# Operand sums of an MLP's first products taken in two column parts, and a token tile's transposes moved in among matmuls

## The chip, the core and the metric

The kernel runs on one NeuronCore of a Trainium2 chip. The engines are TensorE (PE, with its weight loads shown as PEld), VectorE (DVE), ScalarE (ACT) and GpSimd (POOL); SyncE (SP) issues the DMAs. Each engine works through its own queue in order and waits on semaphores for the others. The metric is device time in microseconds of one execution, median of several runs; lower is better.

## What is computed

One encoder layer over 1024 tokens of width 1024, all float32. The part that matters here is the end of the mixing stage and the start of the MLP:

```
x = x + (gate_a * y_a + gate_b * y_b) @ w_out
h = rmsnorm(x, norm_mlp_g)
x = x + square(relu(h @ w_ff1)) @ w_ff2        # w_ff1: 1024 x 4096
```

After the MLP a gated per-layer embedding is added and the result is normalised.

## The kernel before, in words

Every float32 product is made from three matmuls of a reduced-precision pair: `split` (lines 234 to 236) writes a rounded high part on ACT and the remainder, the low part, on DVE, and `mm3` (lines 241 to 248) does high x high, high x low and low x high.

**End of the mixing stage** (`mix_outputs`, from line 973). The gated sum `m` (1024 channels, transposed) is multiplied by `w_out` for eight token tiles of 128 tokens. A tile takes 48 matmuls (eight k-steps of six). Then DVE adds the residual (line 1050), SP stores it (`s_x`), and `scale` (line 1026) normalises the rows: a square with row sums on ACT (line 264), a chain of twelve 128x1 operations on DVE (lines 265 and 253 to 258), and a scaled copy on DVE (line 1028) into a tile of `fx`. `turn(t)` (line 1030) transposes that scaled tile with eight matmuls into PSUM (line 1034), and two copies on ACT (line 1036) spread it over four buffers `hf`, which hold h transposed: f11 and f21 are the first and second half of the channels for tokens 0 to 511 (tiles 0 to 3), f12 and f22 the same for tokens 512 to 1023 (tiles 4 to 7). `turn(t - 1)` is written behind the matmuls of tile t, and `turn(7)` behind everything.

Low and high parts of `w_out` rows 4 to 7 stand in slots 0 to 3 of the six-slot ring `wc`; slots 4 and 5 are unused in this stage.

**Start of the MLP** (`up`, from line 1062). h @ w_ff1 is done by a Winograd scheme of seven half-size products for each job of 256 columns (16 jobs). On the weight side `early` (line 144) loads a job's weights, takes four sums s1 to s4 on POOL (lines 151 to 154) and splits the job's own left half, s1 and s2; `late` (line 160) splits s3, s4 and one more quarter. Splits go to `wc`, which `up` takes in the order of slots 0 to 5. On the side of h the operands are the splits of f11 and f21 (b11, b21; buffers `ha`), of f22 and of f12 - f11 (b22, t1; `hb`), and of three further sums (t2, t3, t4; `hc`). The sums are taken in place, over all 512 columns of a buffer at once:

```
f11 = f12 - f11   (DVE, line 1096)      f22 = f22 - f11   (DVE, line 1101)
f12 = f22 - f12   (POOL, line 1099)     f21 = f22 - f21   (DVE, line 1104)
```

Products 1 and 2 need b11 and b21, product 5 t1, product 6 t2, 7 t3, 3 b22, 4 t4. The first two jobs, a and b, are interleaved: products 1 and 2 of a, of b, then 5 of both, then 6 of both (lines 1106 to 1109), then the rest of a and of b. `ha`, `hb` and `hc` lie over the buffers `m`, `rwt` (the split `m` tiles) and `wo` plus `fx` of the mixing stage, and come free when those do.

**What orders the work.** The kernel is written in program order; a planner assigns each engine's queue before the run. [...] Once planned, a queue is fixed: an instruction that waits holds back everything behind it on its engine. A block `tc.manual_schedule(engines={PE})` keeps PE's instructions of that block in the order in which they are written.

Of the kernel before, what the change touches and what calls it, by code (L numbers as in the profile page):

```python
# [14 lines left out]
ALU = mybir.AluOpType  # L15
# [5 lines left out]
NT = S // P  # L21
KD = D // P
# [203 lines left out]
class Layer:  # L226
# [79 lines left out]
    def run(self):  # L306
        tc, nc, io = self.tc, self.nc, self.io
        base = Region(tc, "base", F32, "left")
        self.ident = base.take(128)
        make_identity(nc, self.ident)  # L310
        self.small = base.ring(8, 16)
        self.bg = base.take(16)
        self.rq = base.take(64)
        self.qss = base.take(64)
        self.qtmp = base.take(64)
        raw = base.take(4096)
        self.raw = Ring([raw[:, 1024 * i:1024 * i + 1024] for i in range(4)])
        self.raw2 = Ring([raw[:, 2048 * i:2048 * i + 2048] for i in range(2)])
        self.gain = base.ring(1, 1024)
        self.g_ring = Ring([base.take(1024), self.gain.slots[0]])  # L320
        pad = Region(tc, "pad", F32, "right")
        pad.take(8)
        psum = Region(tc, "psum", F32, None, space=bass.MemoryType.PSUM)
        self.psum = psum.take(4096)
        self.bank = [self.psum[:, i * 512:(i + 1) * 512] for i in range(8)]
        self.bank2 = [self.psum[:, i * 1024:(i + 1) * 1024] for i in range(4)]

        self.mix_inputs()
        self.attend_a()
        self.mix_outputs()  # L330
        self.wg, self.rg = [], []
        self.up()
        self.down()
        self.ple()
        pad.close()
        psum.close()
        base.close()
# [635 lines left out]
    def mix_outputs(self):  # L973
        tc, nc, io = self.tc, self.nc, self.io
        rm, rwt, wo0 = (Region(tc, n, d, "left") for n, d in (("m", F32), ("rwt", F32R), ("wo", F32R)))
        self.left = [rm, rwt, wo0]
        m = v3(rm.take(8192), KD)
        wt = rwt.ring(8, 1024)
        wo = [(wo0.take(1024), wo0.take(1024)) for _ in range(4)]
        fg = Region(tc, "fg", F32, "right")  # L980
        g_ring = fg.ring(4, 1024)
        ps_r = Ring(self.bank2)
        for c in range(KD):
            wa = self.w_chunk(io["w_out_a"][0], c * P, wt)
            raw = v3(self.raw.next()[:, :256], 2)
            self.load(raw, io["w_out_b"][0][:, c * P:(c + 1) * P].rearrange("(k p) c -> p k c", p=P))
            wb = wt.next()
            wb = [v3(wb[:, 256 * i:256 * i + 256], 2) for i in range(2)]
            self.split(wb[0], wb[1], raw)
            ga, gb = g_ring.next(), g_ring.next()  # L990
            self.load(ga, self.dr["gd"][c])
            self.load(gb, self.dr["gd"][KD + c])
            nc.scalar.activation(ga, ga, AF.Sigmoid)
            nc.scalar.activation(gb, gb, AF.Sigmoid)
            ya, yb = ps_r.next(), ps_r.next()
            for k in range(2):
                self.mm3([yb[:, 0:512], yb[:, 512:1024]], (wb[0][:, k, :], wb[1][:, k, :]),
                         [tuple(self.oB[i][:, k, h * 512:(h + 1) * 512] for i in range(2)) for h in range(2)],
                         k == 0, k == 1)
            self.proj_T(ya, wa, self.oA)  # L1000
            nc.vector.tensor_tensor(out=ga, in0=ga, in1=ya, op=ALU.mult)
            nc.vector.tensor_tensor(out=gb, in0=gb, in1=yb, op=ALU.mult)
            nc.vector.tensor_tensor(out=m[:, c, :], in0=ga, in1=gb, op=ALU.add)
        fg.close()
        self.ro.close()

        self.rc = Region(tc, "rc", F32R, "right")
        self.rf = [Region(tc, n, F32, "right") for n in ("rfa", "rfb")]
        fx = Region(tc, "fx", F32, "right")
        self.wc = self.rc.ring(6, 2048)  # L1010
        self.hf = [self.rf[i].take(2048) for i in (0, 1, 1, 0)]
        hf = [v3(a, 4) for a in self.hf]
        self.rs = self.rf[1].take(1024)
        x_ring = fx.ring(4, 1024)
        gm = self.gain.next()
        self.gain_row(gm, io["norm_mlp_g"][0])
        for k in range(KD):
            if k >= 4:
                s = self.wc.next()
                wo.append((s[:, :1024], s[:, 1024:]))  # L1020
            raw = self.raw.next()
            self.load(raw, io["w_out"][0][k * P:(k + 1) * P, :])
            self.split(wo[k][0], wo[k][1], raw)
        ps_m, ps_t = Ring(self.bank2[:2]), Ring(self.bank2[2:])

        def scale(t, x, xs):
            r = self.row_rstd(x, xs)
            nc.vector.scalar_tensor_tensor(xs, x, r, gm, op0=ALU.mult, op1=ALU.mult)

        def turn(t, xs):  # L1030
            sl = slice(t % 4 * P, t % 4 * P + P)
            ps = ps_t.next()
            for k in range(KD):
                nc.tensor.transpose(ps[:, k * P:(k + 1) * P], xs[:, k * P:(k + 1) * P], self.ident)  # L1034
            for i in range(2):
                nc.scalar.activation(hf[2 * i + t // 4][:, :, sl], v3(ps[:, 512 * i:512 * i + 512], 4), AF.Copy)

        for t in range(NT):
            sl = slice(t * P, (t + 1) * P)
            x, xs = x_ring.next(), x_ring.next()  # L1040
            self.load(x, io["x"][0, sl, :])
            mt = [v3(wt.next(), KD) for _ in range(2)]
            for k in ((slice(0, 7), slice(7, 8)) if t < 2 else (slice(0, 8),)):
                self.split(mt[0][:, k, :], mt[1][:, k, :], m[:, k, sl])
            ps = ps_m.next()
            for k in range(KD):
                self.mm3([ps[:, 0:512], ps[:, 512:1024]], (mt[0][:, k, :], mt[1][:, k, :]),
                         [tuple(w[:, h * 512:(h + 1) * 512] for w in wo[k]) for h in range(2)],
                         k == 0, k == KD - 1)
            nc.vector.tensor_tensor(out=x, in0=x, in1=ps, op=ALU.add)  # L1050
            self.load(self.dr["x1"][sl, :], x)
            scale(t, x, xs)
            if t:
                turn(t - 1, last)
            last = xs
        turn(NT - 1, last)
        fx.close()
        for region in self.left[::-1]:
            region.close()


    def up(self):
        tc, nc, io = self.tc, self.nc, self.io
        w1 = io["w_ff1"][0]
        left = []
# [1 line left out]
        def pair_tile(name, n):  # L1067
            region = Region(tc, name, F32R, "left")
            left.append(region)
            return [tuple(v3(region.take(2048), 4) for _ in range(2)) for _ in range(n)]  # L1070

        b11, b21 = pair_tile("ha", 2)
        b22, t1 = pair_tile("hb", 2)
        t2, t3, t4 = pair_tile("hc", 3)
        f11, f12, f21, f22 = (v3(a, 4) for a in self.hf)
        tiles = [a[:, o:o + 1024] for a in (self.hf[i] for i in (0, 3, 1, 2)) for o in (0, 1024)]
        s_hf, s_own = tiles[6:], [self.g_ring.slots[0], self.rs]
# [6 lines left out]
        def job(j):  # L1084
            return j, w1[:, 256 * j:256 * j + 256], relu2, 1

        v = nc.vector
        n_pair = FF // 256
        wi = Winograd(self, Ring([x[:, o:o + 1024] for x in self.wc.slots for o in (0, 1024)]), Ring(self.bank),
                      Ring(tiles[:6]), lambda j: s_hf if j and j % 2 == 0 else s_own,  # L1090
                      {1: b11, 2: b21, 3: b22, 4: t4, 5: t1, 6: t2, 7: t3}, a22_units=2)
        self.split(*b11, f11)
        self.split(*b21, f21)
        x0 = wi.early(*job(0)[:2])
        wi.late(*x0)
        v.tensor_tensor(out=f11, in0=f12, in1=f11, op=ALU.subtract)
        self.split(*t1, f11)
        x1 = wi.early(*job(1)[:2])
        nc.gpsimd.tensor_tensor(out=f12, in0=f22, in1=f12, op=ALU.subtract)
        self.split(*b22, f22)  # L1100
        v.tensor_tensor(out=f22, in0=f22, in1=f11, op=ALU.subtract)
        self.split(*t2, f22)
        self.split(*t3, f12)
        v.tensor_tensor(out=f21, in0=f22, in1=f21, op=ALU.subtract)
        self.split(*t4, f21)
        a, b = wi.pair(0, x0[2], relu2), wi.pair(1, x1[2], relu2)
        for which in (1, 2), (5,), (6,):
            a.mm(*which)
            b.mm(*which)
        a.first()  # L1110
        b.first()
        wi.late(*x1)
# [232 lines left out]
```

## Time and profile before

| | us |
|---|---|
| median of 3 runs | 1818.11 (1815.13 to 1819.92) |
| the profiled execution, its own time | 1816.29 |
| its span in the trace | 1814.5 |
| PE busy in it | 1746.4 (96%) |
| DVE, ACT, POOL busy | 1244.1, 798.4, 425.9 |

PE's busy time counts overlapping matmuls and modelled ends, so a back-to-back stream is read from the starts of its rows, not from their lengths. In a timeline row the two first numbers are start and duration in us; rows merge neighbours of one form (x is how many), and the bracket is the idle time of that engine just before, with what ended it. [...]

### The profile page before, as it was taken

The numbers are of one execution on the slowest core, as the hardware profiler recorded it, in microseconds if no ns is written. First come the engines' busy times: TensorE is split into PE (matmuls) and PEld (weight loads), VectorE is DVE, ScalarE is ACT, GpSimd is POOL, SyncE is SP. The second block draws the span as 40 slices with busy tenths as digits, with TensorE's granted clock in tenths as the row PEclk, the third lists the DMA queues.
The fourth block names the chain that finished last, engine by engine and source line by source line (L and its number), as shares of the span: only waits on it lengthen the run. The fifth ranks groups of instructions, "written<-read, shape, count | busy, mean of one in ns | idle before, by whom it ended". The sixth has DMA issues, their size and how long they took to land.

```text
span 1814.5 us, 22763 instructions
## 1 busy us (share of the span) xinstructions
PE 1746.4 (96%) x8451; PEld 1438.5 (79%) x8451; DVE 1244.1 (69%) x2055; ACT 798.4 (44%) x1383; POOL 425.9 (23%) x236
## 2 busy tenths in 40 slices
PE   6999999998998899999999989999999999989897
PEld 5888888776787788888888778888888888867786
DVE  7556654466764787875445686555569999999564
ACT  6333233366333677775232445353446333332331
POOL 0242332001000000000001134343337676572000
PEclk9999999999999999999999989999999999999899
DMA  6243234565162322215433214332454333331101
GB/s 215 80 162 122 93 128 140 165 217 178 52 182 66 74 41 22 33 19 140 155 128 118 90 61 140 115 114 97 139 207 152 114 106 113 132 128 35 35 36 47
DMA packets 132287, 199.20 MB, mean 110 GB/s; under 512 B 25508, under 2 KB 92932, under 8 KB 132176
## 3 DMA queue, kind: packets, MB, share of 16 engines
q1 hardware_dynamic: 131008, 194.17, 33.5%
q0 software_dynamic: 1168, 3.57, 0.7%
q8 instruction: 67, 1.10, 0.3%
q14 instruction: 44, 0.36, 0.1%
HBM read 146.12 MB, written 54.73 MB: 111 GB/s over the span
## 4 chain that ended last, share of the span: by engine, by line
PE 52%; DVE 13%; issue 2%; ACT 1%; DMA 0%; DVEq 0%; SPq 0%; ACTq 0%
PE psum L239 48%; DVE rc L236 6%; DVE facc L1178 4%; PE psum L910 3%; DVE fsum L1199 1%; DVE rg L236 1%; DVE hb L236 0%; PE psum L275 0%; PE psum L1034 0%; DVE fsum L1224 0%; ACT fp L904 0%; DVE facc L1213 0%; DVE base L900 0%; DVE fy L273 0%; DMA s_qd<-fa 0%
## 5 line engine op out<-in xcount | busy, mean ns | idle before, releaser
L239 PE MATMUL psum<-rc,rc 128*128 128x512 f32 x1464 | 341.9, 394 | 9.2 <-DVE rc L236 8.8
L239 PE MATMUL psum<-rh,rh 128*128 128x512 f32 (+1 forms) x1428 | 337.4, 389 | 1.6 <-ACT rh L235 1.1
L239 PEld LDWEIGHTS psum<-rc,rc 128*128 128x128 f32 x1464 | 278.2, 190 | 69.1 <-DVE rc L236 9.9
L239 PEld LDWEIGHTS psum<-rh,rh 128*128 128x128 f32 x1428 | 261.1, 190 | 59.6 <-issue 5.9
L151 POOL TENSOR_TENSOR base<-base 128x512 f32<-128x512 f32 x17 | 29.7, 1747 | 711.6 <-DMA base<-in_w_ff 534.5
L239 PE MATMUL psum<-ht,rh 128*128 128x512 f32 x624 | 145.7, 389 | 0.0
L239 PE MATMUL psum<-hc,rc 128*128 128x512 f32 x576 | 137.9, 389 | 0.0
L239 PEld LDWEIGHTS psum<-ht,rh 128*128 128x128 f32 x624 | 117.1, 188 | 24.3
L235 ACT ACTIVATE rh<-base 128x512 fp32r<-128x512 f32 (+1 forms) x77 | 61.2, 808 | 148.3 <-PE psum L239 120.5
L239 PEld LDWEIGHTS psum<-hc,rc 128*128 128x128 f32 x576 | 108.1, 188 | 22.5
L236 DVE TENSOR_TENSOR rh<-base,rh 128x512 fp32r<-128x512 f32 (+1 forms) x77 | 77.6, 1017 | 63.8 <-PE psum L239 39.0
L235 ACT ACTIVATE rc<-base 128x1024 fp32r<-128x1024 f32 (+1 forms) x64 | 51.5, 827 | 151.8 <-PE psum L239 147.3
L239 PE MATMUL psum<-ro,rwt 128*128 128x512 f32 x480 | 109.4, 389 | 0.0
L239 PE MATMUL psum<-kv,rq 128*128 128x512 f32 x384 | 101.3, 400 | 6.0 <-ACT rq L235 4.2
L900 DVE TENSOR_REDUCE base<-psum 128x1 f32<-128x1024 f32 x64 | 78.4, 1224 | 39.0 <-PE psum L239 37.5
L239 PEld LDWEIGHTS psum<-ro,rwt 128*128 128x128 f32 x480 | 90.0, 188 | 18.6
L239 PE MATMUL psum<-rp,kv 128*128 128x512 f32 x384 | 104.4, 406 | 0.0
L209 DVE TENSOR_TENSOR fw<-fw,psum 128x512 f32<-128x512 f32 x91 | 74.4, 817 | 43.2 <-PE psum L239 42.2
L239 PE MATMUL psum<-hb,rc 128*128 128x512 f32 x384 | 94.5, 396 | 5.4 <-DVE hb L236 5.4
L1178 DVE TENSOR_TENSOR facc<-facc,psum 128x1024 f32<-128x1024 f32 x84 | 98.7, 1206 | 0.7 <-PE psum L239 0.7
L236 DVE TENSOR_TENSOR rc<-fsum,rc 128x1024 fp32r<-128x1024 f32 x56 | 95.5, 1730 | 5.1 <-ACT rc L235 5.1
L235 ACT ACTIVATE rc<-fsum 128x1024 fp32r<-128x1024 f32 x56 | 57.4, 1054 | 83.7 <-issue 78.3
(271 smaller groups left out, 3053.7 us busy)
## 6 DMA issues: line engine op xcount, KB each, us to landing
base<-in_w_ff SPq DMA_DIRECT2D x20, 1024.0 KB, 5.5
base<-in_w_in SPq DMA_DIRECT2D x13, 1024.0 KB, 5.1
s_u<-rfa SPq DMA_DIRECT2D x22, 512.0 KB, 2.6
base<-in_w_in SPq DMA_DIRECT2D x20, 512.0 KB, 4.7
fg<-s_gd SPq DMA_DIRECT2D x16, 512.0 KB, 6.0
rfa<-s_u SPq DMA_DIRECT2D x8, 1024.0 KB, 4.9
fraw<-in_w_ff SPq DMA_DIRECT2D x8, 1024.0 KB, 5.5
s_gd<-fw SPq DMA_DIRECT2D x14, 512.0 KB, 3.0
```

What stands on the lines that cost most here:

```text
L151: g.tensor_tensor(out=s1, in0=a21, in1=a22, op=ALU.add)
L209: self.nc.vector.tensor_tensor(out=self.c[out], in0=self.c[a], in1=self.p[i], op=op)
L235: self.nc.scalar.activation(hi, src, AF.Copy)
L236: (eng or self.nc.vector).tensor_tensor(out=lo, in0=src, in1=hi.bitcast(F32), op=ALU.subtract)
L239: self.nc.tensor.matmul(out, lhsT=lhsT, rhs=rhs, start=start, stop=stop)
L900: nc.vector.tensor_reduce(out=nm, in_=ps, axis=AX.X, op=ALU.max, negate=True)
L910: nc.tensor.transpose(pp[:, j * P:(j + 1) * P], probs[j][:, kc * P:(kc + 1) * P], self.ident)
L1178: v.tensor_tensor(out=o, in0=o, in1=ps, op=ALU.add)
L1199: eng.tensor_tensor(out=o, in0=o, in1=acc[i][:, p], op=ALU.add)
```

## The change

The transposes of tile t - 1 move from behind tile t's 48 matmuls to between its k-steps 4 and 5, and PE's order in each tile is kept as written. The transposes of tile 7 move into `up`, behind products 1 and 2 of job a and product 1 of job b. The sums on h's side, and the splits of t1 and b22, are made in two parts: columns 0 to 383 (tiles 4 to 6 against 0 to 2) ahead of `late` of job 0, columns 384 to 511 behind tile 7's transposes. f12 = f22 - f12 goes from POOL to DVE. `up` takes the slots of `wc` in the order 4, 5, 0, 1, 2, 3. t2, t3 and t4 are allocated after tile 7's transposes.

```diff
@@ mix_outputs
-            for k in range(KD):
-                self.mm3([ps[:, 0:512], ps[:, 512:1024]], (mt[0][:, k, :], mt[1][:, k, :]),
...
+            with tc.manual_schedule(engines={mybir.EngineType.PE}):
+                for k in range(KD):
+                    if t and k == 5:
+                        turn(t - 1, last)
+                    self.mm3([ps[:, 0:512], ps[:, 512:1024]], (mt[0][:, k, :], mt[1][:, k, :]),
...
             nc.vector.tensor_tensor(out=x, in0=x, in1=ps, op=ALU.add)
             self.load(self.dr["x1"][sl, :], x)
             scale(t, x, xs)
-            if t:
-                turn(t - 1, last)
             last = xs
-        turn(NT - 1, last)
-        fx.close()
...
+        return fx, lambda: turn(NT - 1, last)
@@ up
-        t2, t3, t4 = pair_tile("hc", 3)
...
-        wi = Winograd(self, Ring([x[:, o:o + 1024] for x in self.wc.slots for o in (0, 1024)]), Ring(self.bank),
...
+        wi = Winograd(self, Ring([x[:, o:o + 1024] for x in self.wc.slots[4:] + self.wc.slots[:4] for o in (0, 1024)]),
...
+        def sums(c):
+
+            x11, x12, x21, x22 = (a[:, :, c] for a in (f11, f12, f21, f22))
+            v.tensor_tensor(out=x11, in0=x12, in1=x11, op=ALU.subtract)
+            self.split(*(a[:, :, c] for a in t1), x11)
+            self.split(*(a[:, :, c] for a in b22), x22)
+            v.tensor_tensor(out=x12, in0=x22, in1=x12, op=ALU.subtract)
+            v.tensor_tensor(out=x22, in0=x22, in1=x11, op=ALU.subtract)
+            v.tensor_tensor(out=x21, in0=x22, in1=x21, op=ALU.subtract)
+
         self.split(*b11, f11)
         self.split(*b21, f21)
         x0 = wi.early(*job(0)[:2])
+        sums(slice(0, 384))
         wi.late(*x0)
-        v.tensor_tensor(out=f11, in0=f12, in1=f11, op=ALU.subtract)
-        self.split(*t1, f11)
         x1 = wi.early(*job(1)[:2])
...
         a, b = wi.pair(0, x0[2], relu2), wi.pair(1, x1[2], relu2)
-        for which in (1, 2), (5,), (6,):
-            a.mm(*which)
-            b.mm(*which)
+        with tc.manual_schedule(engines={mybir.EngineType.PE}):
+            a.mm(1, 2)
+            b.mm(1)
+            turn()
+            fx.close()
+            t2, t3, t4 = pair_tile("hc", 3)
+            wi.operand.update({4: t4, 6: t2, 7: t3})
+            sums(slice(384, 512))
+            b.mm(2)
+            for x, y in (t2, f22), (t3, f12), (t4, f21):
+                self.split(*x, y)
+            a.mm(5)
+            b.mm(5)
+            a.mm(6)
+            b.mm(6)
```

## Rows read from the trace of the kernel before

**Rows 1.** The page's busy time, share of the span and instructions, by engine.

```profile
PE 1746.4 (96%) x8451; PEld 1438.5 (79%) x8451; DVE 1244.1 (69%) x2055; ACT 798.4 (44%) x1383; POOL 425.9 (23%) x236
```

**Rows 2.** Timeline of PE, last mixing tile to product 6 of job a.

```profile
1034.16 6.83 PE L239 MATMUL psum<-ha,rc 128*128 128x512 f32 x29
1044.49 1.61 PE L1034 MATMUL psum<-base,fx 128*128 128x128 f32 x8 [3.50 <-DVE fx L1028]
1045.76 5.80 PE L239 MATMUL psum<-ha,rc 128*128 128x512 f32 x19
1051.39 0.61 PE L239 MATMUL psum<-hb,rc 128*128 128x512 f32 x2
1057.37 7.42 PE L239 MATMUL psum<-hb,rc 128*128 128x512 f32 x22 [5.36 <-DVE hb L236]
1064.62 8.32 PE L239 MATMUL psum<-hc,rc 128*128 128x512 f32 x36
1072.78 2.88 PE L239 MATMUL psum<-hb,rc 128*128 128x512 f32 x12
```

**Rows 3.** Windows 1045.5 to 1047 and 605.5 to 607: engines' busy time, then PEclk, DMA, GB/s.

```profile
1045.50:1047.00 1.50, 1.50 (x6) 1.31 (x5) 1.08 (x1) 1.21 (x3) 0.00 (x0) 0.50 0.87 287
...
605.50:607.00 1.50, 1.50 (x10) 1.23 (x9) 0.77 (x1) 1.08 (x3) 0.00 (x0) 1.00 0.00 0
```

**Rows 4.** Timeline of all engines, first three mixing tiles.

```profile
951.85 5.60 PE L239 MATMUL psum<-wo,rwt 128*128 128x512 f32 x24
...
954.91 1.28 POOL L151 TENSOR_TENSOR base<-base 128x512 f32<-128x512 f32 x1 [504.83 <-DMA base<-in_w_ff]
955.05 1.16 DVE L256 TENSOR_TENSOR base<-base 128x1 f32<-128x1 f32 x1
...
958.74 0.16 DVE L256 TENSOR_TENSOR base<-base 128x1 f32<-128x1 f32 x1
958.77 1.29 POOL L154 TENSOR_TENSOR rfb<-base,base 128x512 f32<-128x512 f32 x1
...
960.89 1.28 DVE L1028 SCALAR_TENSOR_TENSOR fx<-fx,base,base 128x1024 f32<-128x1024 f32 x1
962.09 1.22 DVE L236 TENSOR_TENSOR rc<-base,rc 128x1024 fp32r<-128x1024 f32 x1
...
974.50 1.03 PE L1034 MATMUL psum<-base,fx 128*128 128x128 f32 x8
974.70 1.22 DVE L1050 TENSOR_TENSOR fx<-fx,psum 128x1024 f32<-128x1024 f32 x1 [5.46 <-PE psum L239]
...
979.71 1.28 DVE L1028 SCALAR_TENSOR_TENSOR fx<-fx,base,base 128x1024 f32<-128x1024 f32 x1
```

**Rows 5.** Timeline of all engines, from the last mixing tile on.

```profile
1029.48 2.35 ACT L235 ACTIVATE rc<-base 128x1024 fp32r<-128x1024 f32 x3 [5.13 <-PE psum L239]
...
1032.92 3.48 DVE L236 TENSOR_TENSOR rc<-rfb,rc 128x512 fp32r<-128x512 f32 x2
...
1038.22 0.38 SPq L232 DMA_DIRECT2D base<-in_w_ff  x1
...
1048.35 4.61 POOL L1099 TENSOR_TENSOR rfb<-rfa,rfb 128x2048 f32<-128x2048 f32 x1 [9.06 <-DVE rfa L1096]
1048.71 8.60 DVE L236 TENSOR_TENSOR hb<-rfa,hb 128x2048 fp32r<-128x2048 f32 x2 [0.50 <-ACT hb L235]
...
1061.64 2.28 DVE L236 TENSOR_TENSOR hc<-rfa,hc 128x2048 fp32r<-128x2048 f32 x1
...
1068.97 0.69 DVE L236 TENSOR_TENSOR rc<-base,rc 128x512 fp32r<-128x512 f32 x1 [2.85 <-PE psum L239]
```

**Rows 6.** Timeline of DVE, tile 4.

```profile
1003.03 2.28 DVE L236 TENSOR_TENSOR ha<-rfa,ha 128x2048 fp32r<-128x2048 f32 x1
1005.24 1.28 DVE L1028 SCALAR_TENSOR_TENSOR fx<-fx,base,base 128x1024 f32<-128x1024 f32 x1
```

**Rows 7.** Timeline of PE, a short wait earlier in the kernel.

```profile
604.48 1.65 PE L239 MATMUL psum<-kv,rq 128*128 128x512 f32 x6 [0.70 <-ACT fp L904]
```

More of the change, by code (lines that the diff above doesn't have):

```diff
@@ L329, in run @@
         self.attend_a()
-        self.mix_outputs()
+        fx, turn = self.mix_outputs()
         self.wg, self.rg = [], []
-        self.up()
+        self.up(fx, turn)
         self.down()
@@ L1045, in mix_outputs @@
             ps = ps_m.next()
-            for k in range(KD):
-                self.mm3([ps[:, 0:512], ps[:, 512:1024]], (mt[0][:, k, :], mt[1][:, k, :]),
-                         [tuple(w[:, h * 512:(h + 1) * 512] for w in wo[k]) for h in range(2)],
-                         k == 0, k == KD - 1)
+            with tc.manual_schedule(engines={mybir.EngineType.PE}):
[3 more added lines that the diff above has]
+                    self.mm3([ps[:, 0:512], ps[:, 512:1024]], (mt[0][:, k, :], mt[1][:, k, :]),
+                             [tuple(w[:, h * 512:(h + 1) * 512] for w in wo[k]) for h in range(2)],
+                             k == 0, k == KD - 1)
             nc.vector.tensor_tensor(out=x, in0=x, in1=ps, op=ALU.add)
@@ L1052, in mix_outputs, with up @@
             scale(t, x, xs)
-            if t:
-                turn(t - 1, last)
             last = xs
-        turn(NT - 1, last)
-        fx.close()
         for region in self.left[::-1]:
             region.close()
-    def up(self):
+        return fx, lambda: turn(NT - 1, last)
+    def up(self, fx, turn):
         tc, nc, io = self.tc, self.nc, self.io
@@ L1088, in up @@
         n_pair = FF // 256
-        wi = Winograd(self, Ring([x[:, o:o + 1024] for x in self.wc.slots for o in (0, 1024)]), Ring(self.bank),
-                      Ring(tiles[:6]), lambda j: s_hf if j and j % 2 == 0 else s_own,
-                      {1: b11, 2: b21, 3: b22, 4: t4, 5: t1, 6: t2, 7: t3}, a22_units=2)
+        wi = Winograd(self, Ring([x[:, o:o + 1024] for x in self.wc.slots[4:] + self.wc.slots[:4] for o in (0, 1024)]),
+                      Ring(self.bank), Ring(tiles[:6]), lambda j: s_hf if j and j % 2 == 0 else s_own,
+                      {1: b11, 2: b21, 3: b22, 5: t1}, a22_units=2)
+        def sums(c):
[6 more added lines that the diff above has]
+            v.tensor_tensor(out=x21, in0=x22, in1=x21, op=ALU.subtract)
         self.split(*b11, f11)
@@ L1094, in up @@
         x0 = wi.early(*job(0)[:2])
+        sums(slice(0, 384))
         wi.late(*x0)
-        v.tensor_tensor(out=f11, in0=f12, in1=f11, op=ALU.subtract)
-        self.split(*t1, f11)
         x1 = wi.early(*job(1)[:2])
[L1099 to L1105, printed above, removed]
-        a, b = wi.pair(0, x0[2], relu2), wi.pair(1, x1[2], relu2)
-        for which in (1, 2), (5,), (6,):
-            a.mm(*which)
-            b.mm(*which)
+        a, b = wi.pair(0, x0[2], relu2), wi.pair(1, x1[2], relu2)
+        with tc.manual_schedule(engines={mybir.EngineType.PE}):
[13 more added lines that the diff above has]
+            b.mm(6)
         a.first()
```

## The prediction

> **What bounds the kernel now.** First the busy shares: PE is busy for 96% of the span and DVE, next, for 69% [rows 1], so time is won only where PE stands still. Then PE's timeline from the last mixing tile on [rows 2]; the reader is to look at the brackets. The first product starts at 1034.16, which I call T. 29 matmuls run, PE waits 3.50 us for the last tile's scaled copy, runs its transposes and 19 matmuls, waits 5.36 us for a split into `hb`, and begins product 6 of job a (`hc`) at 1064.62 = T + 30.46. From there matmuls follow without a gap: 36 of them in 1072.78 - 1064.62 = 8.16 us, 0.2267 us each.
>
> That gives the most the seam can return. Up to T + 30.46 PE ran 72 matmuls (16.32 us) and eight transposes, which I put at 0.79 us (of the 22.65 us from 951.85 to 974.50 [rows 4], 96 matmuls take 21.76, and tile 0's transposes the rest, 0.8 to 0.9). 30.46 - 17.11 = 13.35 us are lost: 8.86 us of waits and 4.5 us of slow matmuls. [...] One such loss can be priced: after the 3.50 us wait, 0.79 us of transposes and 19 matmuls (4.31 us) should have ended at 1044.49 + 5.10 = 1049.59, and the next product starts at 1051.39 [rows 2]. So 3.5 us of waiting cost 1.8 us more in clock.
>
> **The change, part by part.**
>
> *Transposes inside a tile.* PE now reaches the transposes of tile t - 1 after 30 matmuls of tile t, 6.80 us behind the end of tile t - 1, and no longer after 48 (10.88 us). In an undisturbed tile the copy of line 1028 ends 979.71 + 1.28 = 980.99, 6.49 us after tile 2's matmuls ended at 974.50 [rows 4]. It fits by 0.3 us: cost nothing, and if that cover goes PE waits at each tile.
>
> Tile 0 is not undisturbed. Job 0's weights land while its chain runs, and POOL takes its four sums from 954.91 to 960.06; meanwhile four of DVE's 128x1 operations last about 1.16 instead of 0.16 us [rows 4]. The copy ends at 960.89 + 1.28 = 962.17. Before, PE asked for it at 951.85 + 10.88 = 962.73; now it asks at 951.85 + 6.80 = 958.65. Nothing ahead of those loads and sums moves, so I expect a **wait of 3.5 us**, priced above at 5.3 us with its clock; behind it in PE's queue stand the tile's last 18 matmuls and all that follows. Also, slots 4 and 5 of `wc` are free, so job 0's first splits no longer wait for PE (before, ACT did so until 1029.48 [rows 5]) and DVE may take them amid that chain: up to 1.22 us for the low part of 128x1024 [rows 4]. I take half: **+5.9 us**. Bounds: 5.3 and 6.5 if the wait is there, 0 if the planner sees it and fills it with matmuls of the next tile.
>
> Tile 4 met the split of b11: 2.28 us of DVE stood in front of its line 1028, which ended at 1006.52 [rows 6], 2.2 us late. With the transposes of tile 3 now 4 us earlier, that split lands ahead of or early in the same chain; bounds 0 and 1.9 us (2.2 less the cover of 0.3). I take **+0.3 us**, near the lower end, since the split also starts earlier.
>
> *The seam.* What has DVE to do before product 6 of a can start? A low part or a subtraction takes 2.28 us for 2048 columns [rows 6] and 0.69 for 512 [rows 5]; a part of 384 columns of four channel blocks (1536) then takes 1.75, one of 128 columns (512) 0.69. The list:
> - low parts of job 0's s3, s4 and last quarter, 3 x 0.69 = 2.1
> - first part of the sums: four subtractions, low parts of t1 and b22, 6 x 1.75 = 10.5
> - tile 7: residual 1.22 [rows 4], twelve small operations 0.19 apart 2.3, scaled copy 1.28 = 4.8
> - job 1's low parts: own half 1.22, four of 0.69 = 4.0
> - second part of the sums, 6 x 0.69 = 4.1
> - t2's low part, 2.28
>
> Together 27.8 us. The first can start when `wo` 4 has been read for the last time (18 matmuls and the transposes before T, 4.9 us) and ACT has rounded s3, about 4.2 us before T; without a gap t2 is ready at T + 23.6. Before, t2 was ready at 1061.64 + 2.28 = T + 29.8, with POOL's 4.61 us f12 sum in the way of b22's split (8.60 us for two splits of 2.28 [rows 5]); that sum is now on DVE and in my list. POOL's s3 and s4 of job 1 still fall there: two 128x512 splits beside such sums took 3.48 instead of 1.38 us [rows 5], so 0 to 3 us, I take 2. And DVE must run dry once, between the last operation that needs no tile 7 and the copies behind tile 7's transposes, and while ACT rounds t2: 1 to 3 us, I take 1.8. So product 6 of a starts at about **T + 27.4**, between T + 24 and T + 30: a **gain of 3.1 us** (0.5 to 6.5), far from 13.35, since DVE's list, not the transposes, sets that point.
>
> Where PE waits meanwhile is job b's product 1: its weights are split into slot 2, which tile 7 reads at k-step 6, and in program order all first-part sums stand ahead. PE gets there at T + 5.4; behind that wait stand tile 7's transposes and all later products. The slow clock after it runs while PE would wait for DVE anyway; for a last wait just short of product 6 I add **+0.7 us** (0 to 1.8).
>
> Costed at nothing: ACT's rounding (the same columns, in two parts); the PSUM banks (job b's product 1 takes one that line 1050 has to free, which stands ahead of job 1's splits on DVE); and SP, whose load for job 2 [rows 5] now waits for a low part behind the sums, up to some 12 us longer, to about 1050. The store of tile 7 shares that queue and PE needs neither soon: job 2's first product comes eight products (21.8 us) behind product 6 of a.
>
> **Sum.** 5.9 + 0.3 - 3.1 + 0.7 = +3.8 us on the profiled execution's 1816.29, so 1820.1 us. That execution lies 1.8 us under the median 1818.11; the difference is put on the median: **1821.9 us**, +0.2%. A measurement of this kernel tells about 0.3%, 5.4 us, from no change; the forecast is inside.
>
> **Rivals.**
>
> *Sums in tile 7's way (slower).* The planner puts large operations among a chain's small ones, as it did with b11's split [rows 6]. If two first-part sums and job 1's splits (1.75 + 1.75 + 4.0 = 7.5 us) all go between tile 7's small operations, its copy ends near T + 17; then come 0.8 of transposes, ACT copies and second part, t2, and product 6 of a starts at T + 29.5, a gain of 1, with 2.5 us of slow clock that nothing covers: 5.9 + 0.3 - 1.0 + 2.5 = +7.7, **1825.8 us**. It decides once the copy ends past about T + 14. For it: the order of the program; against it: the other chains ran unbroken, tile 2's in 6.49 us [rows 4].
>
> *Waits filled (faster).* Each tile's order is fixed only inside its own block. If the planner puts tile 2's matmuls ahead of the late transposes, the 5.9 us vanish; if DVE also idles little at the seam (T + 24), the sum is 0.3 - 6.5 = -6.2: **1811.9 us**. For it: the next tile's operands are split long before. [...]
>
> *The clock at every tile.* A wait of 0.70 us at 604.48 left the clock at 1.00 [rows 7, 3], so short waits have cost only themselves. The mechanism here would be six more transposes that miss their cover of 0.3 us, at 1.8 us of clock each: +10.8, **1832.7 us**. [...] The row of the short wait speaks against it.
>
> *No new order.* If PE's waits stay where they were and DVE's queue keeps the late positions for everything, loss and gain are both missing: **1818 us**.
>
> **How the numbers follow.** Forecast 0.46, sums in the way 0.28, waits filled 0.19, clock at every tile 0.03, no new order 0.04. Faster is the filled case without the 0.01 of it that stays within 5.4 us: 0.18. Slower is the second and the clock case, 0.31; the rest, 0.51, is the same. The forecast's own range, from the bounds of the seam and of the first wait, is 1816 to 1824. To leave out no more than 2 in 10 the range goes on to 1811.5 and 1829.
>
> **What would show it.** Right: in the second mixing tile PE waits 3 to 5 us for line 1028, with the clock at 0.50 behind it; later transposes stand between 30 and 18 matmuls without a wait; no 4.6 us sum on POOL; DVE almost without gaps from 4 us before the first product; PE waiting longest at job b's product 1 or at the last transposes; product 6 of a 26 to 29 us after the first product. Wrong: no wait at the first transposes; t2's low part done before T + 23; or waits at every tile's transposes.

## The result and the profile after

The kernel after takes **1829.43 us** (median of 4 runs, 1828.24 to 1833.85), the kernel before in the same session 1816.89 (1815.13 to 1819.92): ratio **1.0073**, 95% interval 1.0055 to 1.0092. The forecast was 1821.9 in a range of 1811.5 to 1829.0; the time lies just above it, on the side of "slower". The profiled execution took 1829.37 us, its span is 1827.6 against 1814.5 before. PE's busy time is 0.6 us longer (answers to [rows 1]), so nearly all of the 13.1 us between the spans is standing still:

```profile
PE 1747.0 (96%) x8451; PEld 1439.1 (79%) x8451; DVE 1243.2 (68%) x2062; ACT 800.7 (44%) x1385; POOL 420.9 (23%) x235
```

Where, PE's timeline tells in three stretches (answers to [rows 2] and to the PE rows of [rows 4]): the mixing tiles, with the loss at their start, the seam, the start of `down`. (The five `wo` matmuls at 956.33 belong to tile 2: the planner has put them ahead of the transposes of tile 0. From here on T is the start of the first product in the kernel at hand, here 1042.55.)

```profile
938.65 5.60 PE L239 MATMUL psum<-wo,rwt 128*128 128x512 f32 x24
...
949.53 5.60 PE L239 MATMUL psum<-wo,rwt 128*128 128x512 f32 x24
954.97 1.52 PE L239 MATMUL psum<-rc,rwt 128*128 128x512 f32 x6
956.33 1.29 PE L239 MATMUL psum<-wo,rwt 128*128 128x512 f32 x5
964.51 1.97 PE L1034 MATMUL psum<-base,fx 128*128 128x128 f32 x8 [6.88 <-DVE fx L1028]
966.13 5.79 PE L239 MATMUL psum<-rc,rwt 128*128 128x512 f32 x18
971.75 4.47 PE L239 MATMUL psum<-wo,rwt 128*128 128x512 f32 x19
...
1042.55 8.32 PE L239 MATMUL psum<-ha,rc 128*128 128x512 f32 x36
1059.65 1.97 PE L1034 MATMUL psum<-base,fx 128*128 128x128 f32 x8 [8.78 <-DVE fx L1028]
1061.27 4.63 PE L239 MATMUL psum<-ha,rc 128*128 128x512 f32 x12
1065.74 5.62 PE L239 MATMUL psum<-hb,rc 128*128 128x512 f32 x24
1071.20 8.32 PE L239 MATMUL psum<-hc,rc 128*128 128x512 f32 x36
...
1359.52 0.39 PE L239 MATMUL psum<-rc,rc 128*128 128x512 f32 x1
1364.78 269.13 PE L239 MATMUL psum<-rc,rc 128*128 128x512 f32 x1179 [4.87 <-DVE rc L236]
```

The reader is to subtract starts. From tile 0's first matmul to the first product: 1042.55 - 938.65 = 103.90 us, before 1034.16 - 940.97 = 93.19, so **+10.7**. From the first product to product 6 of a: 28.65, before 30.46 [rows 2], so **-1.8**. From there to `down`'s first matmul 288.32 in both; from that to the end 468.08, before 461.56, so **+6.5**. Tile 0 itself began 2.3 us earlier, which is not put down to the change: executions whose work ahead of tile 0 is the same differ by more there (last section). Together +13.1, the difference of the spans. The third stretch is one of which the prediction said nothing.

Rows of other engines' timelines say what PE waits for in the first stretch. ACT, in order, holds job 0's rounding ahead of tile 0's square (line 264) and waits there for weights:

```profile
952.27 1.06 ACT L235 ACTIVATE rc<-base 128x1024 fp32r<-128x1024 f32 x1 [1.93 <-DMA base<-in_w_ff]
953.24 1.04 ACT L264 ACTIVATE fx<-fx 128x1024 f32<-128x1024 f32 x1
```

and DVE has job 0's splits (`rc<-base`) between tile 0's small operations, two of which take 1.0 and 1.1 us beside POOL's sums (one is shown):

```profile
953.37 1.39 DVE L236 TENSOR_TENSOR rc<-base,rc 128x1024 fp32r<-128x1024 f32 x1 [1.28 <-ACT rc L235]
954.68 0.14 DVE L265 TENSOR_SCALAR base<-base 128x1 f32<-128x1 f32 x1
954.92 1.53 DVE L236 TENSOR_TENSOR rc<-base,rc 128x512 fp32r<-128x512 f32 x1
956.38 0.14 DVE L253 TENSOR_SCALAR base<-base 128x1 int32<-128x1 int32 x1
958.30 1.20 DVE L236 TENSOR_TENSOR rc<-base,rc 128x512 fp32r<-128x512 f32 x1 [1.78 <-ACT rc L235]
...
959.60 1.04 DVE L256 TENSOR_TENSOR base<-base 128x1 f32<-128x1 f32 x1
...
963.17 1.28 DVE L1028 SCALAR_TENSOR_TENSOR fx<-fx,base,base 128x1024 f32<-128x1024 f32 x1
```

The copy ends at 964.45, 14.9 us behind tile 0's last matmul (949.53), where an undisturbed one takes 6.5 [rows 4]. At the seam DVE's timeline shows the same pattern, large operations between the small ones:

```profile
1049.48 0.14 DVE L265 TENSOR_SCALAR base<-base 128x1 f32<-128x1 f32 x1
1049.55 1.74 DVE L236 TENSOR_TENSOR hb<-rfa,hb 128x1536 fp32r<-128x1536 f32 x1
1051.21 0.14 DVE L253 TENSOR_SCALAR base<-base 128x1 int32<-128x1 int32 x1
...
1051.94 1.74 DVE L1098 TENSOR_TENSOR rfa<-rfa,rfa 128x1536 f32<-128x1536 f32 x1
...
1058.31 1.28 DVE L1028 SCALAR_TENSOR_TENSOR fx<-fx,base,base 128x1024 f32<-128x1024 f32 x1
```

Tile 7's copy ends at 1059.59, T + 17.0.

### The profile page after: what moved, and what is told of

It reads as the page before. It is cut to its first block, busy times and chain, and to the rows that moved or that the text cites. A ratio compares the mean times of both kernels' runs of the same rounds, so it can differ in the third digit from the quotient of the medians.

```text
span 1827.6 us, 22769 instructions
## 1 busy us (share of the span) xinstructions
PE 1747.0 (96%) x8451; PEld 1439.1 (79%) x8451; DVE 1243.2 (68%) x2062; ACT 800.7 (44%) x1385; POOL 420.9 (23%) x235
## 4 chain that ended last, share of the span: by engine, by line
PE 51%; DVE 13%; issue 2%; ACT 1%; DMA 1%; POOL 0%; SPq 0%; DVEq 0%; ACTq 0%; POOLq 0%
PE psum L239 46%; DVE rc L236 5%; DVE facc L1191 3%; PE psum L910 3%; DVE fsum L1212 1%; DVE rg L236 1%; PE psum L1034 0%; DMA base<-in_w_ff 0%; PE psum L275 0%; DVE fsum L1237 0%; DVE fx L1028 0%; DVE base L258 0%; DVE base L256 0%; DVE fx L1053 0%; POOL fsum L1162 0%
## 5 line engine op out<-in xcount | busy, mean ns | idle before, releaser
L236 DVE TENSOR_TENSOR rc<-fsum,rc 128x1024 fp32r<-128x1024 f32 x56 | 100.0, 1810 | 7.1 <-ACT rc L235 7.1
L239 PE MATMUL psum<-rg,rc 128*128 128x512 f32 x384 | 92.8, 394 | 0.0
```

Source lines behind the costliest of these rows:

```text
L236: (eng or self.nc.vector).tensor_tensor(out=lo, in0=src, in1=hi.bitcast(F32), op=ALU.subtract)
L239: self.nc.tensor.matmul(out, lhsT=lhsT, rhs=rhs, start=start, stop=stop)
```

## The experiments

Below, "mixing" is the time from tile 0's first matmul to the first product, "seam" from there to product 6 of a, "rest" from `down`'s first matmul to the end of the span, all read from PE's timeline as above, each from one profiled execution. How far such a stretch repeats, the kernels tell that don't differ in it: mixing 103.1 to 104.7 us (after, E1, E5, E7), seam 27.6 to 28.9 (after, E1, E4, E6, E10, E12), rest 468.0 to 470.3 (after, E3 to E7, E10, E12) and 458.2 to 459.3 with E1's edit (E1, E8, E9, E11). Smaller differences are not read as effects. The time between seam and rest is 288.3 us in every kernel but E11, where PE waits 0.78 us behind the first two matmuls of product 6. Times are medians; the kernel before, run beside them, was at 1817.51 (E1 to E4), 1816.16 (E5 to E8), 1816.60 (E9 to E11) and 1816.54 (E12).

```
kernel                          mixing   seam    rest    time us   ratio [95%]
before                           93.19   30.46  461.56
after                           103.90   28.65  468.08   1829.43   1.0073 [1.0055, 1.0092]
E1  down on free slots          104.68   28.91  458.65   1823.16   1.0031 [1.0020, 1.0043]
E2  old ring order               99.04   31.17  461.37   1823.68   1.0035 [1.0021, 1.0050]
E3  before + new ring order     100.13   26.75  468.05   1826.51   1.0056 [1.0036, 1.0075]
E4  first transposes later       96.18   27.55  470.10   1824.92   1.0043 [1.0028, 1.0058]
E5  tile 7's copy first         103.91   28.07  469.02   1830.62   1.0081 [1.0066, 1.0096]
E6  tile 0's copy first          97.33   27.88  467.99   1826.10   1.0054 [1.0041, 1.0068]
E7  x21 late                    103.11   26.13  470.30   1831.33   1.0083 [1.0069, 1.0098]
E8  four repairs                 95.06   26.17  458.51   1810.98   0.9969 [0.9960, 0.9978]
E9  + t1 before x22              95.24   24.94  459.32   1808.13   0.9953 [0.9938, 0.9967]
E10 E6 + POOL's sums behind      98.26   28.62  468.62   1825.92   1.0046 [1.0030, 1.0061]
E11 E9 + POOL's sums behind      97.99   22.14  458.15   1811.91   0.9973 [0.9963, 0.9983]
E12 E10 + ACT's roundings behind 95.29   28.90  468.93   1824.50   1.0038 [1.0026, 1.0050]
```

**E1. The wait at `down`.** Theory: up's ring now starts at slot 4, so its last job ends in slots 4, 5, 0, 1, and `down`, which goes on from slot 4 as before, must wait until PE has read that job. In the kernel after, ACT's timeline has that wait ahead of `down`'s first rounding (in the kernel before it ran at 1333.07, without one):

```profile
1345.89 1.07 ACT L235 ACTIVATE rc<-base 128x1024 fp32r<-128x1024 f32 x1 [1.85 <-PE psum L239]
```

```diff
         nb = FF // 512
+        self.wc.i += 4
         x = self.x = st
```

> The kernel after, with one edit at the head of down: the ring wc is stepped on by four half turns, so that down's first splits write the two slots that the last job of up does not occupy. Nothing else moves. Theory (the changed starting slot of up's ring makes down's first splits wait until PE has read the last job's weights): the 4.87 us wait of PE at down's first products is gone, from job 2's first product to the end the time is that of the kernel before within 0.5 us, 6.5 us less than after, about 1823 us. Rival (down starts late because up's last job ends late on ACT and DVE, whatever the slots): the wait stays above 4 us and the time at 1829. Mixing stage (first mixing tile to first product) and seam (first product to product 6 of job a) as in after: 103.9 and 28.65 us within 0.5.

PE's timeline now has no bracket at `down`:

```profile
1362.55 17.62 PE L239 MATMUL psum<-rc,rc 128*128 128x512 f32 x77
```

1823.16 as expected: 6.3 us less than after. The 4.87 us are the ring's. The theory had the end of the kernel as before within 0.5 us; the rest is 2.9 us shorter; with E1's slots a wait of 2.21 us that before and after have late in the rest (PE's transposes of line 275) is missing too. Why is open.

**E2 and E3. The ring order, taken out and put in alone.**

```diff
-        wi = Winograd(self, Ring([x[:, o:o + 1024] for x in self.wc.slots[4:] + self.wc.slots[:4] for o in (0, 1024)]),
+        wi = Winograd(self, Ring([x[:, o:o + 1024] for x in self.wc.slots for o in (0, 1024)]),
```

(E2 makes this edit to the kernel after, E3 its reverse to the kernel before.)

> The kernel after, with up's weight ring back in its old order (first job's weights in slots 0 and 1, which the last mixing tiles still read), so no rotation. Theory: job 0's first splits must wait again until the last tile has read those slots, so they leave the first tile's chain alone; the first transposes wait 3 to 4.5 us instead of 6.88 (what is left is the four... six sums on POOL, if these go there without the splits, 4.5), down's 4.87 us wait is gone (-6.5 us), and the seam is 1 to 4 us longer than after since job 0's splits now fall into it: about 1820 to 1824 us. Rival (POOL's sums alone, not the splits, hold the first chain): the first wait stays at 6.5 to 7 us and the sum is 1823 to 1827.

> The kernel before, with the rotation of up's weight ring alone (first job's weights in slots 4 and 5, which are free from the start of the mixing tiles). Theory: down's start loses 6.5 us; job 0's splits enter the first tile's chain, its scaled copy ends some 25 us after that tile's start as in after, PE asks for it at 21.8 and waits 3 to 4 us plus 1 to 2 of clock; the seam, relieved of job 0's splits, is 1 to 3 us shorter: 1822 to 1827 us. Rival (the splits only enter the chain because the first part of the sums or the order of the transposes pulls them there): the first chain ends at 21.2 us as before, no wait, and the time is 1820 to 1822.

PE's timeline of E2, then of E3:

```profile
962.95 1.44 PE L1034 MATMUL psum<-base,fx 128*128 128x128 f32 x8 [3.12 <-DVE fx L1028]
...
1060.50 1.97 PE L1034 MATMUL psum<-base,fx 128*128 128x128 f32 x8 [11.15 <-DVE fx L1028]
```

```profile
965.86 1.97 PE L1034 MATMUL psum<-base,fx 128*128 128x128 f32 x8 [3.89 <-DVE fx L1028]
...
1360.52 19.80 PE L239 MATMUL psum<-rc,rc 128*128 128x512 f32 x79 [4.88 <-DVE rc L236]
```

Both theories hold, but for E3's seam, 3.7 us shorter where 1 to 3 were expected. Without the ring order the first wait is 3.12 us; from tile 1's first matmul to tile 2's 16.72 us pass, 5.0 more than the 11.67 of 48 matmuls and eight transposes (predicted for POOL's sums alone: 3.5 and 5.3), and the whole mixing costs +5.85. The ring order adds the other 4.9, and 6.5 at `down`, and gives back some 2.5 at the seam (31.17 against 28.65). Alone it costs 9 us.

**E4. The first transposes later.**

```diff
-                    if t and k == 5:
+                    if t == 2 and k == 2:
+                        turn(0, first)
+                    if t > 1 and k == 5:
...
+            if t == 0:
+                first = xs
```

> The kernel after, with the transposes of tile 0 alone put behind the second k-step of tile 2 (12 matmuls into it) instead of behind the fifth of tile 1; all others stay where they are. PE asks for them some 8 us later than in after. Theory (in the mixing stage only this one wait and the slow clock behind it are lost): the 6.88 us wait and 2.4 us of slow clock go, the mixing stage lasts 94 to 95.5 us instead of 103.9, seam and down as in after: 1819.5 to 1821.5 us. Rival (the late copy of tile 0 shifts work that then stalls later tiles, or the matmuls of tile 2 wait in turn for operands): the mixing stage stays above 99 us, the time above 1824.

Mixing 96.18 instead of 103.90: 7.7 of the 10.7 us hang on this one position. The theory missed on detail (94 to 95.5 expected): waits of 0.92 us at tile 0's transposes and 0.75 at tile 1's are left. The time, 1824.92 and not 1820, is the rival's, but its condition, mixing above 99, did not come; the rest was 2 us longer than in after, though the edit does not touch it.

**E5 and E7. The order on DVE at the seam.**

```diff
+            with tc.issue_after(self.copies[7]):
+                rest(c, x11, x12, x21, x22)
...
-        x1 = wi.early(*job(1)[:2])
+        x1 = wi.early(*job(1)[:2], self.copies[7])
```

(`self.copies` holds the instructions of line 1028 by tile; `rest` is what `sums` does from b22's split on; `early` queues the s1 and s2 splits behind the instruction that it is given. These orders are of one engine's queue and add no wait for another.) E7 moves the `x21` subtraction out of `sums`, in one piece, behind t3's split in program order; on DVE the planner still put it ahead of t2's, at 1068.02.

> The kernel after; on DVE alone, what remains of the sums behind t1's split (b22's split, the other subtractions, both parts) and the s1 and s2 splits of job 1 are queued behind the scaled copy of tile 7. The work is the same, only its order on DVE. Theory (the sums and splits between tile 7's twelve small operations delay its copy, and the last transposes with the 36 matmuls behind them set product 6 of a): the copy ends 7 to 9 us after the first product instead of 17.0, PE waits at most 1 us for it instead of 8.78, and product 6 of a, now set by DVE's list, starts 23 to 27 us after the first product instead of 28.65. Mixing stage and down as in after: 1824 to 1828 us. Rival (DVE's list sets product 6 whatever the order in it): the last transposes come early, but product 6 stays at 28 us or later and the time within 1 us of after.

> The kernel after, with the last subtraction of the sums (x21, needed only by t4) done in one piece behind t3's split instead of in two parts ahead of t2's. Theory (each operation ahead of tile 7's copy in DVE's queue pushes the last transposes): 1.75 us less ahead of the copy and 0.69 behind it; the last transposes come 1.7 us earlier (a wait of 7 instead of 8.78), product 6 of a 1.7 to 2.4 us earlier (26.3 to 27 us after the first product). Rival (the gaps between tile 7's small operations are set by something else, ACT or POOL): the wait stays within 0.5 us of 8.78.

E5's DVE and PE timelines, in order of time:

```profile
1050.81 1.28 DVE L1028 SCALAR_TENSOR_TENSOR fx<-fx,base,base 128x1024 f32<-128x1024 f32 x1
```

```profile
1052.15 1.09 PE L1034 MATMUL psum<-base,fx 128*128 128x128 f32 x8 [1.54 <-DVE fx L1028]
1053.00 3.01 PE L239 MATMUL psum<-ha,rc 128*128 128x512 f32 x12
1061.30 0.80 PE L239 MATMUL psum<-hb,rc 128*128 128x512 f32 x1 [5.29 <-ACT hb L235]
1062.44 8.09 PE L239 MATMUL psum<-hb,rc 128*128 128x512 f32 x23 [0.35 <-DVE hb L236]
1070.36 8.32 PE L239 MATMUL psum<-hc,rc 128*128 128x512 f32 x36
```

The copy comes at T + 9.8, the last transposes wait 1.54 instead of 8.78, and product 6 gains 0.6, which is within the scatter of the seam: **the rival**, but not by its reason. t2's low part is ready at T + 26.0; PE starts product 6 at T + 28.07 because product 5 (24 matmuls) is late: its operand, t1's second part, stands behind 5 us of first-part subtractions that product 5 does not need. The wait has moved from line 1034 to `hb`, and behind it the granted clock (PEclk in the tables of windows, as a share of full speed) was 0.50 (1062 to 1066 us): 23 matmuls took 7.92 us from start to start, 5.21 at 0.2267 each. At the full clock t2 would have come last, so about T + 26, inside the theory's 23 to 27; that is an estimate from these rows.

E7 took 1.75 us out ahead of the copy, and the wait fell by 1.5 to 7.26, product 6 by 2.5 to T + 26.13, as its theory said. Its time, 1831.33, is no better than after's, and the runs don't show why: its rest was 2.2 us longer, and the executions scatter by 5.5 us.

**E6, E10 and E12. Tile 0's copy, one cause after another.** E6 queues job 0's splits on DVE behind tile 0's copy. E10 also lets POOL's sums of job 0 wait for that copy (a wait added on POOL). E12 also queues job 0's roundings on ACT behind tile 0's square.

```diff
-        x0 = wi.early(*job(0)[:2])
+        x0 = wi.early(*job(0)[:2], self.copies[0], True)
```

> The kernel after; on DVE alone, the splits of job 0's own half and of its s1 and s2 are queued behind the scaled copy of tile 0. POOL's sums are not moved. Theory (the splits that the free ring slots let in account for some 3.7 us of the first wait, POOL's sums for the 3.1 that the kernel with the old ring order keeps): the first wait falls from 6.88 to 3 to 4 us, the mixing stage lasts 98.5 to 100 us instead of 103.9; seam and down as in after: 1823.5 to 1825.5 us. Rival (POOL's six sums hold the chain alone): the wait stays above 6 us.

> The kernel after with job 0's splits behind tile 0's scaled copy, and POOL's sums of job 0 held back until that copy is done as well. Nothing of job 0 is left in tile 0's chain on DVE or POOL. Theory (the splits made 3.9 us of the first wait of 6.88, POOL's sums beside the small operations about 2, ACT's late square about 1.5): with the splits alone moved the wait was 2.97; it now falls to 0.5 to 1.5 us, all of it from ACT. Rival (POOL's sums are the whole rest): below 0.3 us. Other rival (POOL has no part in it, the small operations are slow beside something else): the wait stays near 3. The mixing stage 94 to 96 us (97.33 with the splits alone moved), unless the sums fall into tile 1's chain, which would show as a wait of 0.5 us or more at the second transposes. Seam and down as in after: 1823 to 1825 us.

> The kernel with job 0's splits and POOL's sums behind tile 0's scaled copy; now job 0's roundings on ACT are queued behind tile 0's square too. Theory (what was left of the first wait, 2.21 us, is ACT's queue: the rounding of job 0 stands ahead of tile 0's square and waits there 2.6 us for its weights to land): the square starts right behind the residual, the copy ends 6.5 us after tile 0's last matmul instead of 9.1, and the first wait is gone (0 to 0.3 us). What is taken out of tile 0's chain may show at the second transposes (1.44 us before). Mixing stage 94 to 96.5 us, seam and down as in after. Rival (the rest of the wait has nothing to do with ACT's order): the wait stays above 1.5 us.

PE's timeline of E6, of E10 and of E12 (in E10 and E12 line numbers are one higher):

```profile
961.79 1.09 PE L1034 MATMUL psum<-base,fx 128*128 128x128 f32 x8 [2.97 <-DVE fx L1028]
```

```profile
961.33 1.09 PE L1035 MATMUL psum<-base,fx 128*128 128x128 f32 x8 [2.21 <-DVE fx L1029]
```

```profile
961.94 1.03 PE L1035 MATMUL psum<-base,fx 128*128 128x128 f32 x8
```

6.88, 2.97, 2.21, 0: the wait is taken apart. In E10 the theory missed (0.5 to 1.5 expected), and ACT's timelines of E10 and E12 say why: ACT's late square, put at about 1.5 us there, costs more.

```profile
955.55 1.06 ACT L236 ACTIVATE rc<-base 128x1024 fp32r<-128x1024 f32 x1 [2.58 <-DMA base<-in_w_ff]
956.51 1.04 ACT L265 ACTIVATE fx<-fx 128x1024 f32<-128x1024 f32 x1
```

```profile
956.59 1.06 ACT L265 ACTIVATE fx<-fx 128x1024 f32<-128x1024 f32 x1 [0.65 <-DVE fx L1054]
...
958.66 1.06 ACT L236 ACTIVATE rc<-base 128x1024 fp32r<-128x1024 f32 x1 [0.92 <-DMA base<-in_w_ff]
```

With slots free, ACT no longer waits for PE but for the weights' landing, with tile 0's square behind it. The copy ends behind tile 0's last matmul by 14.9 us in after, 9.9 in E6, 9.1 in E10, 6.2 in E12. So DVE's splits cost 4.4 to 5.1 (ACT's first rounding of job 0's weights came 0.7 us earlier in E6 than in after, counted from tile 0's start), ACT's queue 2.9. POOL's share is between 0.8 (E10 against E6) and 2.0 (in E6 two small operations took 1.21 and 1.13 instead of 0.16), since E10's weights landed 1.3 us later than E6's. What E10 and E12 put off shows at the second transposes (1.44 and 0.99 us): two splits of job 0, which wait for POOL's sums, now stand on DVE ahead of tile 1's residual. So mixing is no shorter in E10 (98.26) than in E6 (97.33). The times of E6 and E10, 1826.10 and 1825.92, lie 0.6 and 0.9 us above their expectations; E12's wait and mixing came out as expected.

**E8, E9 and E11. Putting it together.** E8 has E1, E6, tile 0's transposes behind the last k-step of tile 1, E5 and E7's late x21. E9 makes x22 in one piece behind t1's and b22's second parts and queues t3's split behind t2's:

```diff
-            v.tensor_tensor(out=x22, in0=x22, in1=x11, op=ALU.subtract)
...
+            v.tensor_tensor(out=f22, in0=f22, in1=f11, op=ALU.subtract)
+            with tc.issue_after(self.split(*t2, f22).ins):
+                self.split(*t3, f12)
```

> The kernel after with all four repairs: down starts on the free ring slots; job 0's splits behind tile 0's copy; tile 0's transposes behind the last k-step of tile 1 (where the kernel before has them); the rest of the sums and job 1's s1 and s2 splits behind tile 7's copy; the x21 subtraction behind t3's split. Theory: no wait at the first transposes (copy after 21.2 us, asked after 21.8), mixing stage 93.2 to 94.5 us (before 93.19), product 6 of a 21.5 to 25 us after the first product (before 30.46), down without its 4.87 us wait: 5 to 9 us less than before, 1808 to 1812 us. Rival (the seam is bounded by DVE's list near 27 us whatever its order, and something of the mixing stage's loss stays): 1814 to 1818 us.

> The kernel with the four repairs, and one more change of order: the subtraction x22 is made in one piece behind the second part of t1 and b22 (before, its first part of 1.75 us stood ahead of them), and t3's split is queued behind t2's. Theory (with the last transposes early, PE waits for t1's second part, the operand of product 5, and not for t2's split): product 5 of a starts 1.5 to 2.5 us earlier (it started 17.3 to 18.5 us after the first product), product 6 with it as long as t2 is ready (24 to 25 us after the first product instead of 26.17): about 1.5 us less, 1809 to 1810.5 us. Rival (DVE's whole list sets product 6): product 5 starts earlier, a wait for t2 takes the place of that for t1, product 6 stays within 0.5 us of 26.17.

> The kernel with the four repairs, the new order of x22 and t3, and POOL's sums of job 0 held back behind tile 0's scaled copy. What the two changes of order give is expected to add up: mixing stage 93.2 to 95 us, product 6 of a 24 to 25 us after the first product, down as with the four repairs: 1808 to 1810 us. Rival (POOL's sums, held back, now slow tile 1's chain, whose transposes have 0.3 us of cover): the mixing stage 96 us or more, 1811 us or more.

E8's first transposes, without a wait; then E9's PE timeline at the seam:

```profile
966.01 1.04 PE L1034 MATMUL psum<-base,fx 128*128 128x128 f32 x8
```

```profile
1053.68 0.53 PE L239 MATMUL psum<-hb,rc 128*128 128x512 f32 x1 [1.95 <-ACT hb L235]
1054.83 8.29 PE L239 MATMUL psum<-hb,rc 128*128 128x512 f32 x23 [0.61 <-DVE hb L236]
1062.96 8.32 PE L239 MATMUL psum<-hc,rc 128*128 128x512 f32 x36
```

E8 and E9 are faster than both kernels. E8's time lies in its theory's range, but mixing (93.2 to 94.5 expected) took 95.06 and product 6 (T + 21.5 to 25) came at T + 26.17. E9 takes **1808.13 us, 0.9953 [0.9938, 0.9967] of the kernel before**. That E9 is faster than E8 is not shown: the intervals overlap and the three stretches add up to 579.7 and 579.5 us. What E9's edit does is seen at product 5, which starts at T + 15.7 (E8: 17.3), in E11 too; product 6 comes at T + 24.94, where its theory had it, but E11, with the same waits up to there, begins it at T + 22.14 by a faster clock (last section) and then waits for t2.

In the stretches E9 gains 5.7 us on before: the seam gives 5.5, the mixing tiles take 2, and 2.2 are the shorter rest that E1 found, which is not of this change. The medians lie 8.5 apart; the other 2.8 us are in none of the three stretches (E9's profiled execution is the slowest of its six).

E11's rival held: POOL's sums, put off, delay tile 1's chain, whose transposes wait 3.64 us, mixing 97.99, time 1811.91. As in E10 it is not the small operations that are late (one of them takes 0.50 us, the others 0.15 or 0.16): job 0's splits, waiting for those sums, stand on DVE ahead of tile 1's residual.

## Why the prediction was wrong, step by step

Two terms failed, and with only one of them missed the time would have been inside the range (E1, without the second, took 1823.16): job 0's splits in tile 0's chain, priced at 0.6 us and measured at 4.9, and the end of the weight ring at `down`, put at nothing and measured at 6.5.

- *Transposes inside a tile* cost next to nothing but the first, as predicted: in after the later ones have two waits of 0.23 us.
- *The first transposes, +5.9*: **the step that failed is "I take half" of 1.22 us for job 0's splits in tile 0's chain.** The part about POOL was right (E2: a wait of 3.12 us and 5.0 with its clock, against 3.5 and 5.3). But the free slots let in three low parts, 4.1 us beside POOL's sums (2.4 us in E6, behind the copy), with waits of 1.3 and 1.8 us for ACT ahead of them, and put the rounding that waits for weights ahead of the square on ACT: E2 against after, 4.9 us. The rival "waits filled" came in small part: five matmuls of tile 2 (1.1 us) stand ahead of the late transposes. I had seen that ACT's rounding would come early and priced only DVE's operation. A step that is let go earlier is to be followed on every queue it enters, and to what it waits for next: here the weights' DMA.
- *Tile 4, +0.3*: a wait of 0.23 us, right.
- *The seam, -3.1 + 0.7*: measured -1.8. t2 was ready at 1070.04, T + 27.5, as forecast, in part by luck: t3's low part (2.2 us) went ahead of t2's and was not in the list, and the rest of the list took about as much less. Product 6 came at T + 28.65. That DVE's list sets it and not the transposes was wrong: PE runs without a gap from the last transposes (1059.65) to product 6, though the list is only 1.2 us behind. Nor did PE wait at job b's product 1: the 36 matmuls from 1042.55 run through. The rival "sums in tile 7's way" is what happened: copy at T + 17.0, priced there at T + 17 (with about 10 us of large operations between tile 7's small ones, not 7.5). Its price, a seam of +1.5 with the clock, was too dear: the forecast's -2.4 was nearer in size, the rival right in mechanism. Against it I held that tile 2's chain ran unbroken; since job 0's splits stay out of tile 0's chain in E2 and go into it in after, where slots are free, that row only showed a chain beside which nothing large was ready.
- *The start of `down`, +6.5*: **the other step that failed is a term that is not in the sum at all**, and the largest miss. E1 takes the 4.87 us wait away, and the time falls by 6.3. The ring's new order was read only where it begins. Its end was to be followed too: which slots the last job leaves, and who takes the next.
- *The clock at every tile* did not happen. Its condition, a wait at each tile, hardly came: in after two of 0.23 us. Where short waits stood, in E4 0.92 and 0.75 us, the eight transposes took 1.09 us and the 12 and 18 matmuls behind them 0.24 and 0.23 us each from start to start (0.34 for E5's 23, where the clock was 0.50); behind the 0.70 us of [rows 7] the clock was 1.00 [rows 3]. No run here has a wait at every tile, so what many of them would do to the clock was not tested.

From the forecast's +3.8 to the +15.4 of the three stretches (10.7 - 1.8 + 6.5): the mixing tiles 10.7 instead of 6.2, the seam -1.8 instead of -2.4, `down` 6.5 instead of 0, so 4.5 + 0.6 + 6.5 = 11.6. This is bookkeeping; what shows the causes are E1, E2 and the runs that take the first wait apart.

## What to carry to other kernels

Where a change moves a buffer ring's start, follow the ring to its end and into the next stage, and follow each operation that is let go earlier through every in-order queue to what it waits for next. Where a planner may put large operations between the small ones of a chain, assume that it does as soon as any are ready, and if a late step hangs on the chain, queue the large ones behind it: here this, with the free slots for `down`, a later first transposition and E9's order of the sums, turned +0.7% into -0.5%, of which 2.2 us (0.1%) are the shorter rest. When a wait is taken away, name the next operand that PE asks for before counting the gain: in E5 7 us of waiting at the transposes became 5.6 us two products later.

## What was not expected of the hardware

**The same wait does not always cost the clock.** E9 and E11 wait at the same products for the same time (1.95 and 0.61 us; 1.97 and 0.64). In E9 the 23 matmuls behind take 8.29 us, in E11 5.49. From the first product on both had done the same on PE: a stream of 36 matmuls, a wait of 1.54 (1.53) us, the transposes (from T + 9.86 in both) and 12 matmuls, then these waits, with product 5 from T + 15.66 in both. E11's rows, beside E9's above:

```profile
1054.56 0.50 PE L240 MATMUL psum<-hb,rc 128*128 128x512 f32 x1 [1.97 <-ACT hb L236]
1055.70 5.49 PE L240 MATMUL psum<-hb,rc 128*128 128x512 f32 x23 [0.64 <-DVE hb L237]
```

The tables of windows (us from the span's start and length, then busy times, then the granted clock) of E9 and of E11:

```profile
1056.00:1058.00 2.00, 2.00 (x7) 1.52 (x6) 1.97 (x2) 1.11 (x2) 0.00 (x0) 0.50 0.00 0
```

```profile
1056.00:1058.00 2.00, 2.00 (x10) 1.64 (x10) 1.97 (x2) 1.11 (x2) 0.00 (x0) 1.00 0.00 0
```

What decided between 0.50 and 1.00, the rows don't show. Nor does the length of one wait decide: behind 2.97 us (E6) and 3.64 us (E11) the transposes took 1.09 us and the 18 matmuls behind them 4.22 and 4.20 from start to start, in E6 with the clock at 1.00 (961 to 967 us); behind 3.12 us (E2) they took 1.44 and 5.55, and the clock fell to 0.50 (964 to 966 us). So a price such as my 1.8 us for a wait of 3.5, read where the clock was 0.50 [rows 3], is one outcome of two. The same is seen ahead of tile 0, where the work of E5 and E7 is the same: 16 transposes behind a wait of 2.42 and 2.48 us took 2.26 us in one and 3.39 in the other, with a mean granted clock of 1.00 and 0.98 in the first 100 us (PE's timelines of E5 and E7):

```profile
58.53 2.26 PE L429 MATMUL psum<-base,fw 128*128 128x128 f32 x16 [2.42 <-DVE fw L427]
```

```profile
59.20 3.39 PE L429 MATMUL psum<-base,fw 128*128 128x128 f32 x16 [2.48 <-DVE fw L427]
```

Tile 0 begins at 938.38 in E5 and at 944.04 in E7. Such differences are why stretches and not spans were compared; that the clock makes all of them is not shown.

**Small operations stretch beside POOL, but not all.** In the kernel after, E2 and E6, some of the 128x1 operations of lines 256 to 258, which have two tensor inputs, take 0.9 to 1.2 us beside POOL's sums and 0.16 without; those with one (lines 253, 254, 265) stay at 0.14 to 0.15. Each of the six so long in after and E2 ends within 0.03 us of the end of POOL's operation beside it: in after that of line 256 begins at 959.60 and ends at 960.64, and POOL's ends at 960.61:

```profile
958.90 1.71 POOL L151 TENSOR_TENSOR base<-base 128x512 f32<-128x512 f32 x1
```

With POOL held back (E10, E12) all of tile 0's are at 0.15 or 0.16. Why of the small operations only those with two tensor inputs stretched, the rows don't show.
